# Output-gate columns turned a block later, one tile of queries instead of two, and other costs in the plan of a Fourier and neighbourhood-attention block

## The chip, the cores and the metric

One core of a Trainium2 chip runs the whole kernel in one launch. The metric is the device time in microseconds (us). The kernel before was timed three times; the profile and the trace come from one further, profiled execution.

## The reference

One layer of a diffusion backbone over 1024 positions of width 1024, with 256 context tokens; float32 throughout.

```python
xn = rms_norm(x, g) * (1 + sc_x) + sh_x          # shift, scale and gate from c through w_ada
cn = rms_norm(ctx, g) * (1 + sc_c) + sh_c
f_in, f_gate, q, k, v, na_gate = split(xn @ w_in)
q, k = rms_norm per head of q and k              # 8 heads of 64
f_out  = real(fft2(f_in, positions x channels)) @ w_four * silu(f_gate)
na_out = softmax([window scores + bias, scores on 256 context keys]) @ [v, vc] * silu(na_gate)
out = x + g_x * (concat(f_out, na_out) @ w_out)
```

The scores are taken as q times k in a higher precision than one pass of the matrix engine gives: a value is split into a high part and a low part that both fit the engine's fast 32-bit format, and the products high by high, low by high and high by low are added.

## The kernel before

TensorE (PE) does nearly all products in that split form, so that most of them come as three matmuls. The work runs in these stages:

- **Front** (L235 to L450): x is normalised, turned and modulated; the Fourier gate's products (`pg`, L365) fill PE.
- **Fold stage** (L597 to L632): the Fourier transform over positions is folded. For each of eight blocks `i` of 128 channels, `fold_products(i)` issues the products of that block (L572 to L585), `next(mid)` issues the sums of a block that is `AHEAD` = 2 blocks later on DVE (VectorE) and ACT (ScalarE), and then `gains(n)` is called for the `n` that `GAINS[i]` lists. `gains` sums the output gate c by w_ada: its matmuls (`pgs`, L284) leave the sums of half the columns in four rows of a PSUM bank. At the last step of each half (n = 3 and n = 7) it also copies the bank to SBUF on ACT (`part`, L491), turns it into columns with four matmuls (`pgc`, L494, recorded as eight) and adds the bias on DVE (`gcol`, L496). `gsum`, `pgc` and the next half's `gsum` use the same single bank, so that `gains(4)` comes behind `gcol`. The columns are needed only much later, in `gate_rows` (L1372).
- **Turn to columns** (`turn_columns`, L653): the folded sums are split by ACT and DVE (`ah`, `al`, L109 and L110; `a`, L663) and multiplied by tables (`pp`, L680 to L684). This begins right behind the fold stage.
- **Attention stage** (L1535 to L1590): this is laid out by a planner that runs while the program is built. It keeps a clock `now` and a list of when each engine is free, gives every operation a cost (for example `a_t(n)` for ACT and `d_t(n)` for DVE), and issues instructions in the order in which its own clock lets them start. That order is then fixed for each engine. Sequences for the Fourier rows, the context, the scores (`seq_rows`), the probabilities (`seq_scores`), their products with the values, and the queries and keys (`seq_build`) come first; wherever none of them can go on, one matmul of a long list (`feed`) is issued on PE: for each pair p of heads the projection `project(p)` (`pqkv`, L827), then the gate's `gate_proj(p)` (`png`, L849), and at the end the Fourier half of the output projection (`po`, L1447).
- **End** (L1592 on): the attention half of the output projection (`of`, L1623) and the sums with x (L1627).

What the change touches in the attention stage: `project` copies each projected tile out of PSUM and normalises q and k by head: squares on ACT, sums on DVE, a power on POOL (GpSimd; `n3`, L733), a product on DVE (`n4`, `raw`, L734). When the planner holds four tiles for done, `queries` and `keys` issue transposes on PE (`ptq` L903, `ptk` L917). `queries` then makes, for each head h, `qs1`: the high part in the head's own 64 partitions (ACT, L906) and the low part in the other 64 (DVE, L907); and `qs2`: a copy of the high part (DVE, L203), with zeros in the other 64 partitions. `ks1` holds the keys' high part in all 128 partitions; `ks2` the low part with zeros in the other 64. A tile of scores is `qs1` by `ks1` (L1171) plus `qs2` by `ks2` (L1173). `open_attention` allocates all this once the context is done, and sets the zeros: on POOL L977 and L978, L997, L1001, on DVE L980 to L994. `OP` and `OD` are what the planner holds POOL and DVE for meanwhile. `PRB` is the number of buffers for a tile of scores turned probabilities (`pr`); `EHB` that of the transposed and split probabilities (`eh`, `el`), and how many of their steps may wait for their products.

Of the kernel before, what the change touches and what calls it, by code (L numbers as in the profile page):

```python
# [11 lines left out]
F32 = mybir.dt.float32  # L12
R = mybir.dt.float32r
# [6 lines left out]
P = 128  # L20
# [3 lines left out]
TW, RT0, RT1, RT2, RH = 4, 0, 4, 4, 1  # L24
XS = (4, 8)
LAG, EB, TL = 1, 2, 0
AHEAD, GAINS = 2, ((0,), (1, 2), (3, 4), (5, 6), (7,), (), (), ())
S = dict(sem=0.13, rw=4, wo=2.6, rt=0, ri=12, rf=0, ro=1, ns=3, rr=2, rv=2)
WHO = dict(ml=(1, 0), ol=(0, 1), w=None, cw=(0, 1), ga=None, ce=(1, 0), el=(0,), vl=(0, 1), q2=(0,), kb=(0, 2), fm=None, wc=(2,), ec=(2,), oc=(0, 2), mc=(2, 0), cc=(2, 0), vc=(2,), fe=(0,), gc=(2,))
OP, OD, OC = 4.5, 2.0, 8.0  # L30
SEQ = 1024
CTX = 256
NB = 8
# [9 lines left out]
def tile_hybrid_block(  # L43
# [24 lines left out]
    act, dve, pool, pe = nc.scalar, nc.vector, nc.gpsimd, nc.tensor  # L68
    mm = pe.matmul

    def tap(name, t):
        if name in taps:
            nc.sync.dma_start(out=taps[name], in_=t)

    def f(t):
        return t.bitcast(F32)
# [107 lines left out]
    def a_t(n):  # L184
        return 0.09 + n * 0.00083

    def d_t(n):
        return 0.07 + n * 0.00104
# [11 lines left out]
    def copy_by(n, who, out, in_):  # L200

        both = ((DVE_, dve.tensor_copy, lambda n: 0.07 + n * 0.00052), (POOL_, pool.tensor_copy, p_t), (ACT_, act.copy, a_t))
        return [(e, time(n), lambda cp=cp: cp(out, in_)) for e, cp, time in (both[k] for k in who)]  # L203
# [265 lines left out]
                mm(o, g3[w][:, i], x[i][:, 512:1024], start=(i == 0 and n == 0), stop=(i == KT - 1 and n == 2))  # L469
        act.activation(gate_f[3][:, 512:1024], o, AF.Silu)  # L470

    gws, gsum = [], []

    def load_gains():

# [5 lines left out]
    def gains(n):  # L481
        hf, m = divmod(n, 4)
        if m == 0:
            gsum.append(bank("pgs", 2))
        o = gsum[hf]
        for k in range(2):
            condition(o, 2 * m + k, gws[n][:, k])
        if m < 3:
            return
        part = eop.tile([P, 512], F32, tag="s2", bufs=3, name="part")  # L490
        act.copy(part, o)  # L491
        gc = bank("pgc", 2)
        for j in range(4):
            mm(gc[:, j:j + 1], part[:, j * P:(j + 1) * P], pick[:, 0:1], start=True, stop=True)  # L494
        ks = slice(4 * hf, 4 * hf + 4)
        dve.tensor_tensor(out=gcol[:, ks], in0=gc[:, 0:4], in1=vec[:, V_BG + 4 * hf:V_BG + 4 * hf + 4], op=ALU.add)  # L496
# [92 lines left out]
    def load_table(n):  # L589
        kt, l = divmod(n, 2)  # L590
        t = pwp.tile([P, DM + 2], R, tag="wd", bufs=4, name="tab")
        pool.dma_start(out=t, in_=(tab_h, tab_l)[l][kt * P:(kt + 1) * P, :])
        (tbh, tbl)[l].append(t)
# [3 lines left out]
    with tc.manual_schedule(engines=MANUAL):  # L597
        fold_zero()
        for i in range(EB):
            fold_ends(i)  # L600
        mid = fold_middle()
        for _ in range(6 * AHEAD):
            next(mid)
        for j in range(4):
            fourier_gate(j)
        for n in range(8):
            fold_weights(n // 4, n % 4)
            if n > 3:
                load_gains()
            if n % 4 == 3:  # L610
                fold_nyquist(n // 4)
        last_gate()
        pe_0 = bank("p0", 0)
        pe_e = [bank(f"pe{m}", 1 - m % 2) for m in range(4)]
        pe_o = [bank(f"po{m}", 1 - m) for m in range(2)]
        for i in range(KT):
            fold_products(i)
            for _ in range(6):
                next(mid, 0)
            if i == 1:  # L620
                load_four()
            if i == 5:
                dve.tensor_tensor(out=wfr[0], in0=wfr[0], in1=wfr[1], op=ALU.add)
                dve.tensor_tensor(out=wfr[2], in0=wfr[2], in1=wfr[1], op=ALU.subtract)
            for n in GAINS[i]:
                gains(n)
                if n < 4:
                    load_gains()
                else:
                    load_table(n - 4)  # L630
    tap("gate_f", gate_f[1])
    st4.close()  # L632
    st1.close()
# [176 lines left out]
    def project(p):  # L810
        raws[p] = []
        for t in range(NB):
            while now[0] < banks[0]:
                yield None
            if t % 4 == 0:
                while p and not has(("v", p - 1, 0, t // 4), ("v", p - 1, 1, t // 4)):
                    yield None
                raw = rawp.tile([P, 4, 384], F32, tag="raw", name="raw")
                raws[p].append(raw)
            o = pj("pqkv")[:, 0:384]  # L820
            ts_ = slice(t * P, (t + 1) * P)
            for k in range(KT):
                while ("w", p, k) not in done:
                    yield None
                wh, wl = weights[p][k]
                for n, (x, w) in enumerate(((xnh, wh), (xnh, wl), (xnl, wh))):
                    mm(o, x[k][:, ts_], w, start=(k == 0 and n == 0), stop=(k == KT - 1 and n == 2))  # L827
                    yield 0.16
                if t == NB - 1 and p < 3:
                    prep(p + 1, k)  # L830
            rt = raw[:, t % 4]
            sqt = rawp.tile([P, 256], F32, tag="sqt", name="sqt")
            while t > 1 and ("raw", p, t - 2) not in done:
                yield None
            banks.append(1e9)
            banks.pop(0)
            n1, n2, n3, n4 = head_norm(rt[:, 0:256], sqt, 4)
            chain((ACT_, a_t(384), lambda rt=rt, o=o: act.copy(rt, o), 0),  # L838
                  lambda: banks.__setitem__(0 if banks[0] == 1e9 else 1, clock()),
                  (ACT_, a_t(256), n1), (DVE_, 0.42, n2), (POOL_, 0.96, n3), (DVE_, d_t(256), n4),  # L840
                  lambda t=t: done.__setitem__(("raw", p, t), 1), rank=S["rr"])

    def gate_proj(p):
# [54 lines left out]
    def queries(p, q):  # L898
        cs = slice(512 * q, 512 * q + 512)
        tbs[0] -= 1  # L900
        pq = tb("ptq")
        for j in range(4):
            pe.transpose(pq[:, j * P:(j + 1) * P], raws[p][q][:, j, 0:P], ident)  # L903
        for h in range(2):
            a, b = HALF[h], HALF[1 - h]
            chain((ACT_, a_t(512), lambda h=h, a=a: act.copy(qs1[h][a, cs], pq[a])),  # L906
                  (DVE_, d_t(512), lambda h=h, a=a, b=b: dve.tensor_tensor(out=qs1[h][b, cs], in0=pq[a], in1=f(qs1[h][a, cs]), op=ALU.subtract)),  # L907
                  lambda h=h: give() if h else None,
                  copy_by(512, WHO["q2"], qs2[h][a, cs], f(qs1[h][a, cs])),
                  lambda h=h: done.__setitem__(("q", p, h, q), 1), rank=h)  # L910

    def keys(p, c, cs, srcs):
# [44 lines left out]


    gts, att = ExitStack(), ExitStack()
    gtp = ap1 = ap2 = qs1 = qs2 = ks1 = ks2 = eye = rrow = sel = biases = trs = sms = None  # L960
    PRB, VSB = 5, 1

    def open_attention():
        nonlocal gtp, ap1, ap2, qs1, qs2, ks1, ks2, eye, rrow, sel, biases, trs, sms
        gfs.close()
        pqs.close()
        gst.close()
# [1 line left out]
        ap1 = att.enter_context(tc.tile_pool(name="ap1", bufs=1, **LT))  # L969
        ap2 = att.enter_context(tc.tile_pool(name="ap2", bufs=2, **LT))  # L970
        qs1 = [ap1.tile([P, SEQ], R, name=f"qs1{h}") for h in range(2)]
        qs2 = [ap1.tile([P, SEQ], R, name=f"qs2{h}") for h in range(2)]
        ks1 = [ap1.tile([P, SEQ + CTX], R, name=f"ks1{h}") for h in range(2)]
        ks2 = [ap1.tile([P, SEQ + CTX], R, name=f"ks2{h}") for h in range(2)]
        for h in range(2):
            b = HALF[1 - h]
            pool.memset(f(qs2[h])[b], 0.0)  # L977
            pool.memset(f(ks2[h])[b], 0.0)  # L978
        eye = ap1.tile([104, 8], F32, name="eye")
        dve.tensor_copy(eye, ident[0:104, 0:8])  # L980
# [177 lines left out]
    def row_max(p, h, t):  # L1158
# [8 lines left out]
        for z in range(2):  # L1167
            for o, kk in ((sl, lk), (sc, slice(SEQ, SEQ + CTX))):
                st, sp = (z == 0 and not (edge and o is sc)), (z == 1 and not (edge and o is sl))
                if z == 0:  # L1170
                    mm(o, qs1[h][:, ts_], ks1[h][:, kk], start=st, stop=sp)  # L1171
                else:
                    mm(o, qs2[h][:, ts_], ks2[h][:, kk], start=st, stop=sp)  # L1173
        now[0] += 2 * (nl + CTX) / 2400
        done["s", p, h, t] = 1
        pr = prs[p, h, t] = ap1.tile([P, 640], F32, tag="pr", bufs=PRB, name="pr")[:, 0:nl + CTX]
# [41 lines left out]


    STEPS = (10, 11, 0, 1, 2, 3, 12, 4, 13, 5, 6, 7)  # L1220
    EHB = 3
    pvs = {}

    def turned(p, h, t, kt):
# [324 lines left out]
    def feed():  # L1549
        for k in range(KT):  # L1550
            prep(0, k)
        prep_gate(0)
        for p in range(4):
            yield from project(p)
            if p == 3:
                wst.close()
                yield from gate_rows()
                side.append(out_loads())
            while "open" not in done:
                yield None  # L1560
            yield from gate_proj(p)
            if p < 3:
                prep_gate(p + 1)
        yield from out_fourier()
# [191 lines left out]
```

## Time and profile before

| what | value |
|---|---|
| median of 3 runs | 576.97 us |
| lowest and highest of them | 574.51 and 578.93 us |
| the profiled execution | 575.37 us |
| its span, first to last instruction | 573.6 us |
| matrix engine busy in the span | 546.6 us |
| VectorE, ScalarE, GpSimd busy | 388.5, 312.6, 139.9 us |

An engine's busy time is the union of its instructions. The records of consecutive matmuls overlap, because each is shown until its last result is out; the distance from start to start is what one costs. "Idle before, releaser" of an instruction is the time in which its engine had nothing running, and what it waited for.

### The profile page before, as it was taken

The numbers are of one execution on the slowest core, as the hardware profiler recorded it, in microseconds if no ns is written. First come the engines' busy times: TensorE is split into PE (matmuls) and PEld (weight loads), VectorE is DVE, ScalarE is ACT, GpSimd is POOL, SyncE is SP. The second block draws the span as 40 slices with busy tenths as digits, with TensorE's granted clock in tenths as the row PEclk, the third lists the DMA queues.
The fourth block names the chain that finished last, engine by engine and source line by source line (L and its number), as shares of the span: only waits on it lengthen the run. The fifth ranks groups of instructions, "written<-read, shape, count | busy, mean of one in ns | idle before, by whom it ended". The sixth has DMA issues, their size and how long they took to land.

```text
span 573.6 us, 9000 instructions
## 1 busy us (share of the span) xinstructions
PE 546.6 (95%) x3299; PEld 483.5 (84%) x3299; DVE 388.5 (68%) x801; ACT 312.6 (55%) x662; POOL 139.9 (24%) x144
## 2 busy tenths in 40 slices
PE   4899999999999899999999999999999898989997
PEld 3677896799878889999989999899998687868886
DVE  5774756686754868866678667777765978783142
ACT  6865462355665368764688646767456855520000
POOL 2200000115702533112431032411224513540000
PEclk9999999999999899999999999999999999999999
DMA  8991046426551521110221111220113556120052
GB/s 339 412 408 58 1 148 215 152 89 198 193 147 38 179 65 42 42 43 37 81 66 45 30 49 51 70 70 1 42 46 112 184 191 203 73 92 0 1 201 93
DMA packets 41459, 64.64 MB, mean 113 GB/s; under 512 B 3268, under 2 KB 25156, under 8 KB 40392
## 3 DMA queue, kind: packets, MB, share of 16 engines
q1 hardware_dynamic: 40408, 60.40, 31.1%
q0 software_dynamic: 1008, 3.67, 1.9%
q8 instruction: 26, 0.43, 0.3%
q14 instruction: 17, 0.14, 0.1%
HBM read 55.15 MB, written 8.91 MB: 112 GB/s over the span
## 4 chain that ended last, share of the span: by engine, by line
PE 75%; DVE 8%; ACT 6%; DMA 6%; issue 2%; POOL 2%; SPq 1%; POOLq 0%; DVEq 0%; ACTq 0%
PE pqkv L827 20%; PE of L1623 8%; PE pg L365 7%; PE po L1447 5%; PE st L1251 4%; PE png L849 4%; DMA wr<-in_w_in_dram 3%; PE s L1171 2%; PE s L1173 2%; PE pv L1285 2%; PE pv L1275 2%; DMA x<-in_xb_dram 2%; DMA owr<-in_w_out_dram 2%; PE pc L1133 1%; PE pw L502 1%
## 5 line engine op out<-in xcount | busy, mean ns | idle before, releaser
L827 PE MATMUL pqkv<-wl,xnh 128*128 128x384 f32 x256 | 88.3, 345 | 0.0
L827 PE MATMUL pqkv<-wh,xnl 128*128 128x384 f32 x256 | 88.0, 344 | 0.0
L827 PE MATMUL pqkv<-wh,xnh 128*128 128x384 f32 x256 | 87.8, 343 | 0.0
L733 POOL TENSOR_TENSOR hrs<-hss,mhalf 128x4 f32<-128x4 f32 (+1 forms) x34 | 36.7, 1082 | 149.2 <-DVE hss L730 145.8
L1262 DVE TENSOR_TENSOR el<-st,eh 128x512 fp32r<-128x512 f32 (+2 forms) x96 | 53.5, 572 | 17.0 <-ACT eh L1261 16.3
L1261 ACT CAST eh<-st 128x512 fp32r<-128x512 f32 (+2 forms) x96 | 47.0, 494 | 29.4 <-PE st L1251 25.9
L1183 ACT ACTIVATE pr<-pr,tr 128x640 f32<-128x640 f32 (+1 forms) x64 | 51.5, 805 | 15.4 <-DVE tr L1179 15.1
L1179 DVE CUSTOM_DVE_ANT_0 pr<-s,bias 128x640 f32<-128x640 f32 (+1 forms) x64 | 50.2, 784 | 10.6 <-PE s L1173 10.2
L827 PEld LDWEIGHTS pqkv<-wh,xnh 128*128 128x128 f32 x256 | 48.7, 190 | 0.6
L827 PEld LDWEIGHTS pqkv<-wl,xnh 128*128 128x128 f32 x256 | 48.6, 190 | 0.5
L827 PEld LDWEIGHTS pqkv<-wh,xnl 128*128 128x128 f32 x256 | 48.6, 190 | 0.4
L1251 PE MATMUL st<-ident,pr 128*128 128x128 f32 x304 | 47.3, 272 | 0.1
L1251 PEld LDWEIGHTS st<-ident,pr 128*128 128x128 f32 x304 | 37.0, 140 | 2.8 <-DVE el L1262 0.5
L1447 PE MATMUL po<-oh,mh 128*128 128x512 f32 x88 | 31.0, 396 | 3.0 <-DVE y L1453 1.5
L1627 DVE TENSOR_TENSOR y<-y,of 128x512 f32<-128x512 f32 (+1 forms) x17 | 11.1, 656 | 32.3 <-PE of L1623 32.3
L1171 PE MATMUL s<-ks,qs 128*128 128x256 f32 (+1 forms) x128 | 29.9, 313 | 0.7 <-DVE tr L1179 0.7
L203 ACT CAST wh<-wr 128x384 fp32r<-128x384 f32 (+1 forms) x44 | 22.6, 539 | 12.7 <-DMA wr<-in_w_in_dram 10.6
L1173 PE MATMUL s<-ks,qs 128*128 128x256 f32 (+1 forms) x128 | 28.3, 302 | 0.0
L198 DVE TENSOR_TENSOR wl<-wr,wh 128x384 fp32r<-128x384 f32 (+1 forms) x29 | 21.5, 754 | 9.6 <-ACT wh L203 7.7
L198 POOL TENSOR_TENSOR wl<-wr,wh 128x384 fp32r<-128x384 f32 (+1 forms) x19 | 20.9, 1104 | 28.9 <-ACT wh L203 15.2
L365 PE MATMUL pg<-xnh,w 128*128 128x512 f32 x96 | 27.3, 406 | 0.0
L838 ACT COPY raw<-pqkv 128x384 f32<-128x384 f32 x32 | 15.3, 478 | 21.4 <-PE pqkv L827 21.1
(295 smaller groups left out, 1442.9 us busy)
## 6 DMA issues: line engine op xcount, KB each, us to landing
wd<-in_w_ada_b_dram SPq DMA_DIRECT2D x8, 1024.0 KB, 11.6
wr<-in_w_in_dram SPq DMA_DIRECT2D x40, 192.0 KB, 2.8
wr<-in_w_in_dram SPq DMA_DIRECT2D x24, 256.0 KB, 3.1
x<-in_xb_dram SPq DMA_DIRECT2D x8, 512.0 KB, 7.3
wdg<-in_w_ada_g_dram SPq DMA_DIRECT2D x8, 512.0 KB, 4.7
owr<-in_w_out_dram SPq DMA_DIRECT2D x16, 256.0 KB, 3.4
y<-in_xb_dram SPq DMA_DIRECT2D x8, 512.0 KB, 5.4
out_dram<-y SPq DMA_DIRECT2D x15, 256.0 KB, 2.1
```

Of the source, the lines that this page charges most:

```text
L198: return [(e, time(n), lambda eng=eng: eng.tensor_tensor(out=out, in0=in0, in1=in1, op=op)) for e, eng, time in (both[k] for k in who)]
L365: mm(pg[j][hf], wj, x[i][:, hs], start=(i == 0 and g == 0), stop=(i == KT - 1 and g == 2))
L827: mm(o, x[k][:, ts_], w, start=(k == 0 and n == 0), stop=(k == KT - 1 and n == 2))
L1171: mm(o, qs1[h][:, ts_], ks1[h][:, kk], start=st, stop=sp)
L1173: mm(o, qs2[h][:, ts_], ks2[h][:, kk], start=st, stop=sp)
L1179: dve.tensor_tensor_reduce(out=pr, in0=sv, in1=bt, scale=-1.0, scalar=3.0e38, op0=ALU.add, op1=ALU.min, accum_out=tr[:, t:t + 1])
L1183: (ACT_, a_t(nl + CTX) + 0.15, lambda: act.activation(pr, pr, AF.Exp, bias=tr[:, t:t + 1], scale=-1.0, accum_out=sm[:, t:t + 1]), 1),
L1251: pe.transpose(s[:, j * P:(j + 1) * P], turned(p, h, t, kt), ident)
L1261: chain((ACT_, a_t(m), lambda: act.copy(eh[:, w], s3)), (DVE_, d_t(m), lambda: dve.tensor_tensor(out=el[:, w], in0=s3, in1=f(eh)[:, w], op ...
L1262: (DVE_, d_t(m), lambda: dve.tensor_tensor(out=el[:, w], in0=s3, in1=f(eh)[:, w], op=ALU.subtract)), give,
L1447: mm(o, mf[k][m][:, ts_], wf[hf][k][w_], start=(k == 0 and n == 0), stop=(k == 3 and n == 2))
L1623: mm(o[:, cs], ma[k][m][:, ts_], w[:, cs], start=(k == 0 and n == 0), stop=(k == 3 and n == 2))
```

## The change

The two halves of `gains` are separated: the copy to SBUF stays behind the last sums of a half, and a new `gain_columns(hf)` does the turning and the bias. It is called for the first half at the end of block 3, ahead of `gains(4)`, and for the second half behind block 7. `GAINS` moves n = 4 from block 2 to block 3 and n = 6 from block 3 to block 4. `qs2` is gone, with its copies, its zeros and its memory, and the second product of the scores takes `qs1`. `PRB` goes from 5 to 6 and `EHB` from 3 to 4. The planner's costs: `OP` 4.5 to 3.5, `n3` 0.96 to 1.1, `n4` `d_t(256)` (that is 0.34) to 0.9. In `feed`, the wait of `gate_proj` for `open_attention` is gone.

```diff
-AHEAD, GAINS = 2, ((0,), (1, 2), (3, 4), (5, 6), (7,), (), (), ())
+AHEAD, GAINS = 2, ((0,), (1, 2), (3,), (4, 5), (6, 7), (), (), ())
-OP, OD, OC = 4.5, 2.0, 8.0
+OP, OD, OC = 3.5, 2.0, 8.0
...
             condition(o, 2 * m + k, gws[n][:, k])
-        if m < 3:
-            return
-        part = eop.tile([P, 512], F32, tag="s2", bufs=3, name="part")
-        act.copy(part, o)
+        if m == 3:
+            gpart.append(eop.tile([P, 512], F32, tag="s2", bufs=3, name="part"))
+            act.copy(gpart[hf], o)
+
+    def gain_columns(hf):
+
+        part = gpart[hf]
         gc = bank("pgc", 2)
         for j in range(4):
             mm(gc[:, j:j + 1], part[:, j * P:(j + 1) * P], pick[:, 0:1], start=True, stop=True)
...
             for n in GAINS[i]:
+                if n == 4:
+                    gain_columns(0)
                 gains(n)
...
+        gain_columns(1)
...
-                  (ACT_, a_t(256), n1), (DVE_, 0.42, n2), (POOL_, 0.96, n3), (DVE_, d_t(256), n4),
+                  (ACT_, a_t(256), n1), (DVE_, 0.42, n2), (POOL_, 1.1, n3), (DVE_, 0.9, n4),
...
-                  copy_by(512, WHO["q2"], qs2[h][a, cs], f(qs1[h][a, cs])),
...
-    PRB, VSB = 5, 1
+    PRB, VSB = 6, 1
...
-        qs2 = [ap1.tile([P, SEQ], R, name=f"qs2{h}") for h in range(2)]
...
-            pool.memset(f(qs2[h])[b], 0.0)
...
-                if z == 0:
-                    mm(o, qs1[h][:, ts_], ks1[h][:, kk], start=st, stop=sp)
-                else:
-                    mm(o, qs2[h][:, ts_], ks2[h][:, kk], start=st, stop=sp)
+                mm(o, qs1[h][:, ts_], (ks1, ks2)[z][h][:, kk], start=st, stop=sp)
...
-    EHB = 3
+    EHB = 4
...
-            while "open" not in done:
-                yield None
             yield from gate_proj(p)
```

## Rows read from the trace of the kernel before

**Rows 1.** The page: engines over the span (busy us, share, instructions).

```profile
PE 546.6 (95%) x3299; PEld 483.5 (84%) x3299; DVE 388.5 (68%) x801; ACT 312.6 (55%) x662; POOL 139.9 (24%) x144
```

**Rows 2.** The chain that ended last, its end (start us, us, what).

```profile
506.93 19.36 PE po L1447 x84
526.29 43.71 PE of L1623 x204
```

**Rows 3.** Waits of PE over the span (us in total, times, longest us).

```profile
PE pt L328 <- ACT x L341: 9.3, 2, 7.6
PE ptq L903 <- DVE raw L734: 3.8, 2, 2.4
PE pv L1275 <- DVE el L1262: 2.9, 4, 1.2
...
PE pgc L494 <- ACT part L491: 1.5, 2, 0.7
PE po L1447 <- DVE gate L855: 1.5, 1, 1.5
```

**Rows 4.** Timeline of PE, the second half's columns (start us, us, engine, line, op, [idle before]).

```profile
109.38 1.05 PE L494 MATMUL pgc<-pick,part 128*128 128x1 f32 x8 [0.74 <-ACT part L491]
110.30 0.28 PE L572 MATMUL p<-wab_h,x0h 128*2 128x260 f32 x1
```

**Rows 5.** Timeline of DVE, from the second half's columns to the first splits.

```profile
110.47 0.16 DVE L496 TENSOR_TENSOR gcol<-pgc,vec 128x4 f32<-128x4 f32 x1 [2.01 <-PE pgc L494]
110.55 0.75 DVE L553 TENSOR_TENSOR s<-ef 128x256 f32<-128x256 f32 x2
...
117.71 1.51 DVE L110 TENSOR_TENSOR al<-pe,ah 128x260 fp32r<-128x260 f32 x4 [0.50 <-ACT ah L109]
119.56 0.42 DVE L663 TENSOR_TENSOR a<-a0f,a 2x260 fp32r<-2x260 f32 x1 [0.33 <-ACT a L662]
```

**Rows 6.** Timeline of PE, first products behind the fold stage.

```profile
119.63 0.28 PE L680 MATMUL pp<-tab,ah 128*4 128x258 f32 x1
...
120.42 0.28 PE L684 MATMUL pp<-onesr,a 34*4 34x258 f32 x1
```

**Rows 7.** Timeline of PE: first pair's queries, last projections, the gate's first product.

```profile
191.19 0.49 PE L903 MATMUL ptq<-ident,raw 128*128 128x128 f32 x3
194.05 0.33 PE L903 MATMUL ptq<-ident,raw 128*128 128x128 f32 x1 [2.37 <-DVE raw L734]
...
205.70 0.33 PE L827 MATMUL pqkv<-wh,xnl 128*128 128x384 f32 x1
...
206.40 0.40 PE L849 MATMUL png<-xnh,gh 128*128 128x512 f32 x1
```

**Rows 8.** Windows: stretch; us; PE, PEld, DVE, ACT, POOL busy; granted clock; DMA share; GB/s.

```profile
195.00:198.00 3.00, 3.00 (x12) 3.00 (x12) 2.69 (x5) 1.27 (x2) 0.62 (x1) 0.55 0.41 118
...
430.00:460.00 30.00, 25.55 (x148) 21.66 (x147) 23.98 (x42) 21.93 (x44) 15.04 (x11) 1.00 0.42 141
```

**Rows 9.** Timeline of DVE in `open_attention`.

```profile
188.02 3.27 DVE L982 COPY eye<-ident 8x8 f32<-8x8 f32 x3
...
193.57 0.42 DVE L734 TENSOR_TENSOR raw<-raw,hrs 128x256 f32<-128x256 f32 x1
```

**Rows 10.** Timeline of POOL in `open_attention`.

```profile
188.21 0.95 POOL L977 MEMSET qs<- 64x1024 f32 x1
189.10 1.17 POOL L978 MEMSET ks<- 64x1280 f32 x1
...
192.95 0.19 POOL L1001 MEMSET tr<- 128x40 f32 x2
```

**Rows 11.** Timeline of PE, the last pair's second queries.

```profile
437.63 0.33 PE L903 MATMUL ptq<-ident,raw 128*128 128x128 f32 x1 [1.42 <-DVE raw L734]
```

**Rows 12.** Group by line on DVE (busy us, mean ns, idle before).

```profile
L203 DVE CAST qs<-qs 64x512 fp32r<-64x512 f32 x16 | 7.0, 441 | 0.1
```

**Rows 13.** Waits of PE from 430 to 510.

```profile
PE pv L1275 <- DVE el L1262: 2.3, 2, 1.2
```

More of the change, by code (lines that the diff above doesn't have):

```diff
@@ L470, in last_gate @@
         act.activation(gate_f[3][:, 512:1024], o, AF.Silu)
-    gws, gsum = [], []
+    gws, gsum, gpart = [], [], []
     def load_gains():
@@ L959, in tile_hybrid_block @@
     gts, att = ExitStack(), ExitStack()
-    gtp = ap1 = ap2 = qs1 = qs2 = ks1 = ks2 = eye = rrow = sel = biases = trs = sms = None
-    PRB, VSB = 5, 1
+    gtp = ap1 = ap2 = qs1 = ks1 = ks2 = eye = rrow = sel = biases = trs = sms = None
+    PRB, VSB = 6, 1
     def open_attention():
-        nonlocal gtp, ap1, ap2, qs1, qs2, ks1, ks2, eye, rrow, sel, biases, trs, sms
+        nonlocal gtp, ap1, ap2, qs1, ks1, ks2, eye, rrow, sel, biases, trs, sms
         gfs.close()
```

## The prediction

> **What bounds the kernel now.** I read the engine shares first: PE is busy for 546.6 of 573.6 us and no other engine for more than 388.5 [rows 1]. So PE's queue is the bound and the only question is what stops it. The end of the chain of waits says the same: from 506.93 to 570.00 it is nothing but PE products [rows 2]. Whatever stall goes ahead of that shortens the whole; a chain of the attention that ends earlier gains nothing by itself, because PE still has 19.36 us of `po` products to issue behind it. The change removes no matmul, so it can only gain from the 573.6 - 546.6 = 27.0 us in which PE stands. The list of PE's waits says where [rows 3]: 9.3 us are the wait for the first x, which the change does not touch. What it can touch is `ptq` behind `raw` (3.8), `pv` behind `el` (2.9), `pgc` behind `part` (1.5) and `po` behind the gate (1.5), together 9.7 us. One cost is not in that list: behind the longest `ptq` wait the granted clock was 0.55 over 3 us [rows 8].
>
> **The gate's columns.** In each half PE stands 0.74 us for ACT's copy (1.5 us in two waits) [rows 3, 4]. Behind the change the products of the next block cover that copy, so 0.74 us goes for the first half. The sums only change blocks, at no cost, the DMAs of the tables that `gains` issues on POOL's queue come up to one block later and are needed only behind block 7, and `gains(4)` still follows `gcol`. For the second half 0.74 goes as well, and the eight turning products, 110.30 - 109.38 = 0.92, move behind block 7. So the last fold product ends at 119.63 - 0.74 - 0.74 - 0.92 = 117.23, and the turning products run to 118.15. But the new order also puts `gcol` into DVE's queue, and there the splits `al` and then `a` are behind it. `gcol` started 1.09 us after the first turning product (109.38 to 110.47), and the next DVE instruction 0.08 later [rows 4, 5]: so `gcol` now starts at 118.32 and `al` at 118.40, where it was 117.71. With 1.51 for `al` and 0.42 for `a` [rows 5], `a` is ready at about 120.33, and the product that reads it, which started at 120.42 [rows 6], starts at about 120.35. Of 1.48 us of waits removed 0.1 is left. Ends: 1.5 gained, if DVE's order costs nothing, and 0.5 lost, if `a` comes 0.5 later than I reckon, as much as the idle time that DVE already has there before `al`. I take 0.1, since every link of the chain has a row.
>
> **One tile of queries.** The 16 copies go, 7.0 us of DVE at 441 ns [rows 12], and the two `qs2` zeros of 0.95 us on POOL [rows 10]. The matmuls that took `qs2` take `qs1` and keep their size, because `ks2` is zero where `qs1` has the low part. Where PE is supplied, which is all but the places of its waits [rows 3], the copies lie beside PE's own work and gain nothing. They count at two places.
>
> First, in `open_attention`. The tile that PE waits for from 191.19 on is multiplied by DVE only at 193.57, behind a block of small instructions that begins at 188.02 [rows 7, 9]. Three 8x8 copies in it took 3.27 us, to 191.29, beside the zeros on POOL; zeros of 0.95, 1.17 and 0.95 in a row from 188.21 end at the same time [rows 9, 10]. So the copies get through when the third zero is done. Without `qs2` the first three zeros are two of 1.17 and a `bias` one, for which 0.25 is left (192.95 less the four long ones is 0.5 for two), and end near 190.8: 0.5 sooner. The rest of the block took 193.57 - 191.29 = 2.28, part of it beside zeros too; I put 0.2 on that. So DVE's product comes 0.7 sooner. Ends: nothing, if the copies wait for all that POOL has, and 1.9, if DVE gains what POOL gains.
>
> The Trainium skill, page "SBUF — State Buffer", section "Who interferes with whom", says that a DVE copy in a 2-port mode and a GpSimd instruction lock each other out, whichever comes second for one whole instruction. By that the three copies would have ended at 190.3 (the first ahead of the zeros, the others behind one zero each), one zero earlier than the row has it [rows 9, 10], so the trace shows a longer lock. By the rule the copies would now end at 190.6 behind the second `ks2` zero, DVE would gain 0.9 instead of 0.7, and the sum would be 4.3.
>
> Second, in the last pair, where PE is idle for 30.00 - 25.55 = 4.45 us of 430 to 460 [rows 8]. Four copies are 1.76 us of DVE there. But ACT is as full as DVE (21.93 against 23.98 of 30 us), so DVE's saving mostly turns into waiting for ACT. Ends: 1.8 gained, all of it, and 1.0 lost, if the plan, which now holds the queries for done 0.47 earlier (0.34 for the copy and 0.13 for its semaphore), issues scores before their data. I take 0.5, and 0.3 more for the small `pv` waits of the pairs before, half of 2.9 less the 2.3 of the last pair [rows 3, 13].
>
> **The planner's costs.** `n4` was planned at 0.34 us and took 0.42 [rows 9]; planned at 0.9 it puts the transposes `ptq` 0.56 us later in the plan, behind 0.56/0.16 = 3.5 more projection matmuls. Four of them took 206.40 - 205.70 = 0.70 [rows 7], so 0.6 us of work stands where PE waited. `n3` adds 0.14 us where POOL is not held. In the first pair the wait of 2.37 [rows 7] falls by 0.6 + 0.7 = 1.3; I take 1.2. In the last pair the wait of 1.42 [rows 11] falls by 0.6. The clock: over 195 to 198 it was 0.55, which cost 3 x 0.45 = 1.4 us [rows 8]. The wait of 1.42 in the last pair left the clock at 1.00 over 430 to 460 [rows 11, 8], so a first-pair wait of 1.2 should do so too, and the 1.4 us comes back. Ends: 0, if the fall has another cause, and 1.6. I take 1.4.
>
> **What costs and gains nothing.** `OP` only says when the plan lets POOL go on; POOL's zeros took 192.95 + 0.19 - 188.21 = 4.9 us and will take 3.0, so 3.5 fits as 4.5 did. The wait removed from `feed` was never waited for: the queries, which need the opening, stand at 191.19 and the gate's first product at 206.40, right behind the last projection [rows 7]. That edit is worth 0 unless the opening moves by 15 us. The sixth `pr` and the fourth `eh`, `el` let the attention run further ahead, which only changes which PE work comes first; they take 2.5 + 4 KB of the 8 KB per partition that `qs2` leaves, so nothing is pushed out.
>
> **The sum.** 0.1 (columns) + 1.2 (first queries) + 1.4 (clock) + 0.6 (last queries) + 0.5 (last pair) + 0.3 (small waits) = 4.1 us. The profiled execution took 575.37 with a span of 573.6; it would be 571.3 with a span of 569.5. The median of the runs, 576.97, is 1.6 above it, within their spread (574.51 to 578.93), and I set the forecast against the median: 576.97 - 4.1 = 572.9. One per cent, about what a measurement of this kernel can tell from no change, is 5.8 us.
>
> **The rivals.**
> A: the first wait stays. If the new plan lets the power `hrs` of the fourth tile slip behind POOL's zeros, DVE's `raw` is no earlier than now, the clock falls again, and 1.2 + 1.4 are not gained. For it: the order on POOL is the planner's and its costs changed. Against: the power is done before the zeros now and its cost rises by only 0.14. Time: 576.97 - 1.5 = 575.5.
> B: slower, through the last pair. The plan holds queries for done earlier, and with six and four buffers it puts more reductions and splits ahead of one another; DVE (23.98 of 30 us) and ACT (21.93) are already full there [rows 8], and PE, which takes its instructions in order, stands behind `el` and the gate. For it: that is what the waits of 2.3 (`pv`) and 1.5 (`po`) are now [rows 3, 13]. Against: the copies leave DVE and `n4` is planned too long. If the idle time of 4.45 doubles and the 0.5 is not gained, the time is 576.97 - 3.6 + 4.45 = 577.8; it decides from 3.6 us of new waiting on.
> C: more than forecast. The splits are not held up by `gcol` (1.4 more) and the last pair's waits for `el` and the gate (2.3 + 1.5 = 3.8) go too, 3.3 more than the 0.5 taken: 572.9 - 4.7 = 568.2. For it: `n4` and the copies together give the plan 2 to 3 us per pair of room. Against: ACT in the last pair, and the queue of DVE in the fold stage.
> D: the change does not do what it says: the gate's products do not wait for the attention now. That is in the sum as 0.
>
> **How the numbers follow.** Forecast 0.50, A 0.20, B 0.12, C 0.18. The forecast's own range is 570.5 to 575 (clock or not, last pair between -1 and +1.8). The range of 8 in 10 runs from 567.5 (a little past C) to 578 (B). Faster by over 1% means under 571.2: most of C (0.16) and the lower part of the forecast (0.15), 0.31. Slower by over 1% means over 582.7: B with twice its price, 0.04. The rest, 0.65, is within 1%.
>
> **What would show it.** In the fold stage: no wait of `pgc` for `part`; `gcol` of the second half directly ahead of `al`, and `al` at about 1.2 us behind the end of the last fold product. In the first pair: the wait of `ptq` at 0.9 to 1.5 us and the granted clock at 1.00 behind it. In the last pair: `ptq` under 1 us, and the sum of its waits for `el` and the gate at about 3.3. Busy PE within 2 us of 546.6, DVE down by about 7 us. Wrong I would be if the clock falls again, if `al` does not wait for `gcol`, or if a wait of over 2 us stands at a place where there was none.

## The result, and the profile after

The changed kernel took 571.18 us (median of 4 runs, 567.38 to 572.41) beside 576.94 for the kernel before on the same chip: a ratio of 0.988, 95% interval 0.984 to 0.992, so 5.8 us faster (4.5 to 9.1). The forecast was 572.9. Timed again later, beside 576.11, it took 570.11: 0.989 (0.986 to 0.993).

The profiled execution took 572.41 us with a span of 570.6, only 3.0 us under the one of before. Its engine shares and granted clock, from the page:

```profile
PE 546.2 (96%) x3299; PEld 485.0 (85%) x3299; DVE 377.6 (66%) x788; ACT 311.2 (55%) x659; POOL 140.4 (25%) x142
...
PEclk9899999899999999999999999999999989999999
```

There are three falls of the clock in it: near 20 us, near 105 and near 457. A second profiled execution of the same kernel took 567.87 us, and its page has no fall:

```profile
PE 542.7 (96%) x3299; PEld 481.9 (85%) x3299; DVE 377.5 (67%) x788; ACT 311.5 (55%) x659; POOL 140.4 (25%) x142
...
PEclk9999999999999999999999999999999999999999
```

PE is 3.5 us less busy there with the same instructions. So stages are compared below only where the clock is known. The waits of PE in the first profiled execution, to be held against [rows 3]:

```profile
PE pt L328 <- ACT x L341: 10.4, 3, 7.6
PE pgs L284 <- issue: 1.6, 1, 1.6
...
PE s L1173 <- DVE tr L1179: 1.3, 2, 1.0
...
PE pv L1285 <- DVE el L1262: 1.1, 1, 1.1
PE ptq L909 <- DVE raw L740: 1.1, 2, 0.7
PE pv L1275 <- DVE el L1262: 1.0, 1, 1.0
PE pp L690 <- POOL p L664: 0.8, 1, 0.8
```

`pgc` behind `part` (1.5) and `po` behind the gate (1.5) are gone, `ptq` fell from 3.8 to 1.1. The two lines of `pv` behind `el` have 2.1 together, where before had 2.9; `s` behind `tr` (DVE's step that adds the bias to a tile of scores) rose from 0.7 to 1.3. Two waits are of a new kind, both in the fold stage: 1.6 ahead of `pgs` and 0.8 ahead of `pp`. PE's timeline at the places where the stages meet:

```profile
86.84 0.28 PE L575 MATMUL p<-wab_h,x0h 128*2 128x260 f32 x1
...
102.42 0.95 PE L497 MATMUL pgc<-pick,part 128*128 128x1 f32 x8
...
105.01 1.57 PE L284 MATMUL pgs<-wdg,ccol 128*32 128x512 f32 x8 [1.64 <-issue]
...
121.86 0.28 PE L686 MATMUL pp<-tab,ah 128*4 128x258 f32 x1
...
123.57 0.28 PE L690 MATMUL pp<-onesr,a 34*4 34x258 f32 x1 [0.84 <-POOL p L664]
...
195.13 0.49 PE L909 MATMUL ptq<-ident,raw 128*128 128x128 f32 x3
...
196.32 0.33 PE L909 MATMUL ptq<-ident,raw 128*128 128x128 f32 x1 [0.70 <-DVE raw L740]
...
206.54 0.40 PE L855 MATMUL png<-xnh,gh 128*128 128x512 f32 x1
...
415.42 0.60 PE L909 MATMUL ptq<-ident,raw 128*128 128x128 f32 x4
...
435.13 0.33 PE L909 MATMUL ptq<-ident,raw 128*128 128x128 f32 x1 [0.36 <-DVE raw L740]
...
523.40 0.39 PE L1621 MATMUL of<-oh,mh 128*128 128x512 f32 x1
```

From such starts the time splits as follows (us; (c) marks a stage in which the granted clock fell below 0.9 for some 3 us; the best version is an experiment further down):

| stage, from PE's start to start | before | after | after, second execution | best version |
|---|---|---|---|---|
| span's start to the first fold product `p` | 84.64 | 86.84 (c) | 85.40 | 85.38 |
| to the first `pp` by `onesr`: fold stage | 35.78 | 36.73 (c) | 35.19 | 33.02 |
| to the first `png`: context, first projection and queries | 85.98 (c) | 82.97 | 83.02 | 83.36 |
| to the last pair's first `ptq`: the pairs between | 210.54 | 208.88 | 208.87 | 209.64 |
| to the first `of`: the last pair | 109.19 | 107.98 (c) | 106.39 | 106.33 |
| `of` to PE's end | 43.86 | 43.86 | 43.86 | 43.86 |

The first line of the table is ahead of everything that the change touches and varies by itself. Without it the second execution is 8.0 us shorter than the one of before: 0.6 in the fold stage, 3.0 to the gate's products, 1.7 in the pairs, 2.8 in the last pair. Some of the 3.0 is the fall of the clock that only the profile of before has there.

### The profile page after: what moved, and what is told of

Same layout as the page of the kernel before. It is cut to its first block, busy times and chain, and to the rows that moved or that the text cites. A ratio compares the mean times of both kernels' runs of the same rounds, so it can differ in the third digit from the quotient of the medians.

```text
span 570.6 us, 8972 instructions
## 1 busy us (share of the span) xinstructions
PE 546.2 (96%) x3299; PEld 485.0 (85%) x3299; DVE 377.6 (66%) x788; ACT 311.2 (55%) x659; POOL 140.4 (25%) x142
## 4 chain that ended last, share of the span: by engine, by line
PE 81%; DVE 6%; DMA 4%; ACT 3%; issue 2%; POOL 2%; SPq 1%; POOLq 0%; ACTq 0%; DVEq 0%
PE pqkv L833 20%; PE of L1621 8%; PE pg L365 7%; PE s L1173 6%; PE png L855 6%; PE st L1251 6%; PE po L1447 5%; PE pv L1285 3%; PE pv L1275 2%; DMA wr<-in_w_in_dram 2%; DMA x<-in_xb_dram 2%; PE pc L1136 1%; PE pw L505 1%; PE ada L284 1%; PE pc L1135 1%
## 5 line engine op out<-in xcount | busy, mean ns | idle before, releaser
L833 PE MATMUL pqkv<-wh,xnl 128*128 128x384 f32 x256 | 86.8, 339 | 0.0
L1173 PE MATMUL s<-ks,qs 128*128 128x256 f32 (+1 forms) x256 | 48.0, 309 | 1.3 <-DVE tr L1179 1.3
L1173 PEld LDWEIGHTS s<-ks,qs 128*128 128x128 f32 x256 | 39.5, 188 | 4.0 <-DVE tr L1179 3.0
L198 POOL TENSOR_TENSOR wl<-wr,wh 128x384 fp32r<-128x384 f32 (+1 forms) x19 | 22.1, 1166 | 27.3 <-ACT wh L203 22.5
L1447 PE MATMUL po<-oh,ml 128*128 128x512 f32 x64 | 26.0, 406 | 0.0
```

Of the source, the lines that this page charges most:

```text
L1173: mm(o, qs1[h][:, ts_], (ks1, ks2)[z][h][:, kk], start=st, stop=sp)
L1447: mm(o, mf[k][m][:, ts_], wf[hf][k][w_], start=(k == 0 and n == 0), stop=(k == 3 and n == 2))
```

## Experiments

"Gains" below is the move of the gate's columns, "costs" are `OP`, `n3` and `n4`, "buffers" `PRB` and `EHB`.

### The gate's columns undone, and alone

From the changed kernel:

```diff
-AHEAD, GAINS = 2, ((0,), (1, 2), (3,), (4, 5), (6, 7), (), (), ())
+AHEAD, GAINS = 2, ((0,), (1, 2), (3, 4), (5, 6), (7,), (), (), ())
...
-        if m == 3:
-            gpart.append(eop.tile([P, 512], F32, tag="s2", bufs=3, name="part"))
-            act.copy(gpart[hf], o)
-    def gain_columns(hf):
-        part = gpart[hf]
+        if m < 3:
+            return
+        part = eop.tile([P, 512], F32, tag="s2", bufs=3, name="part")
+        act.copy(part, o)
...
-                if n == 4:
-                    gain_columns(0)
...
-        gain_columns(1)
```

> The changed kernel with the old gains and the old GAINS, all else as changed. Theory: the new order of the gate's columns costs more than it removes, by two waits that come from reused memory. From the first fold product to the first product that reads the zero row (L684 of before, L690 of the changed kernel) the profile of before has 35.79 us and that of the changed kernel 36.72. So here 35.8, and a time 0.9 us under the changed kernel's. Rival: the new order gains what it removes (1.5 us) and the loss in the one profile is chance; then 1.5 us above the changed kernel's.

The reverse of this diff, put into the kernel before:

> The kernel before with the new gains and GAINS alone. Theory (reused memory): the same stretch takes 36.7 instead of 35.8 us, PE stands about 1.6 us ahead of the sums of n = 4 and about 0.8 us ahead of the product that reads the zero row; the time is 0.9 us above that of before, everything behind as before. Rival (it gains 1.5): the stretch takes 34.3 and the time falls by 1.5 us.

Undone: 569.64 us, 0.989 (0.987 to 0.992). Alone: 576.26, 0.999 (0.997 to 1.002). So by time this part is worth nothing that can be measured. By the stage table it is worth 0.6 us: the fold stage has 35.78 before and 35.19 with the new order alone, no fall in either. Both expectations missed that: they took the 36.73 of the first profile for the cost of the order, and that stage has a fall of the clock in it. (With the order undone the stage took 37.34, also with a fall, so that profile can't be used here.) The two new waits were as expected. They are in the timeline after:

```profile
103.47 0.76 DVE L556 TENSOR_TENSOR s<-xrt 128x256 f32<-128x256 f32 x2 [1.64 <-PE pgc L497]
104.15 0.68 DVE L562 TENSOR_TENSOR l<-s,h 128x512 fp32r<-128x512 f32 x1
104.75 0.15 DVE L499 TENSOR_TENSOR gcol<-pgc,vec 128x4 f32<-128x4 f32 x1
...
119.14 1.50 DVE L110 TENSOR_TENSOR al<-pe,ah 128x260 fp32r<-128x260 f32 x4 [0.50 <-ACT ah L109]
...
122.04 0.16 DVE L499 TENSOR_TENSOR gcol<-pgc,vec 128x4 f32<-128x4 f32 x1 [1.39 <-PE pgc L497]
...
122.07 0.31 POOL L661 MEMSET a<- 64x260 f32 x1 [8.91 <-PE pgc L497]
122.10 0.38 ACT L667 ACTIVATE a0f<-p 2x260 f32<-2x260 f32 x1 [1.91 <-PE pgc L497]
...
123.00 0.42 DVE L669 TENSOR_TENSOR a<-a0f,a 2x260 fp32r<-2x260 f32 x1 [0.80 <-ACT a L668]
```

In the first half `part` is one of three buffers of the tag `s2`, and now holds it a block longer. The next fold sum `s` needs that buffer and waits for `pgc`; `gcol` is behind it and behind `l` on DVE; and the sums of `gains(4)` need the bank that `gcol` reads. So PE stands 1.64 us at 105.01, where it stood 0.25 before: 1.39 more, against the 0.74 saved. In the second half `gcol` is not ahead of `al`; it is behind, and `al` is not late. What is late is `a`: ACT's `a0f` and POOL's zeros have no data from `pgc`, yet both are released by it. Both write memory laid out anew where `part` lay. That was a theory so far, and the next kernel tests it.

Together the new waits are 2.2 us longer than the old ones of the same places, more than the 1.48 us that the order removes. The stage is shorter all the same, because the sums themselves take less. From the trace before, one step of the sums (n = 4) and two in one block (n = 5 and 6), each with the fold product behind it:

```profile
99.26 1.05 PE L284 MATMUL pgs<-wdg,ccol 128*32 128x512 f32 x4 [0.25 <-DVE gcol L496]
100.24 0.28 PE L572 MATMUL p<-wab_h,x0h 128*2 128x260 f32 x1
...
103.42 1.06 PE L284 MATMUL pgs<-wdg,ccol 128*32 128x512 f32 x8
104.41 0.28 PE L572 MATMUL p<-wab_h,x0h 128*2 128x260 f32 x1
```

One step takes 0.98 us from start to start, and two steps whose sums go to different rows of the bank take 0.99. Before, the eight steps came in six such groups, since `pgc` stood between n = 3 and n = 4; with the new `GAINS` they come in five, (4, 5) and (6, 7) together. From start to start, waits left out, PE spends 6.06 us on the sums before and 4.95 with the new order (4.95 also in the kernel of the next section). So the 0.6 us are 1.1 us of sums and a few tenths at `pgc`, less the 0.7 by which the waits grew.

### The copy put into memory that nobody waits for

The same computation; `part` goes into a half of x's tile that has been read by then:

```diff
-            gpart.append(eop.tile([P, 512], F32, tag="s2", bufs=3, name="part"))
+            gpart.append(xrt[1][:, 1 + 2 * hf, 512:1024])
```

> The changed kernel with the two copies of the gate's sums in the half of x that the fold has already read, instead of in a buffer of the fold's sums. Theory (reused memory): DVE no longer waits for the turning products before it can write the fold's sums, and ACT and POOL no longer wait for them before they write the zero row's tiles; both new waits go, the first falls to the 0.3 us that the columns' sum takes, and the stretch takes about 34.4 us: 2.3 us less than the changed kernel and 1.4 less than before. My forecast's reason (the sum of the columns stands ahead of the splits on DVE): the first wait goes all the same, but the second stays, and the stretch takes about 35.2.

It took 567.92 us, 0.985 (0.983 to 0.988). The changed kernel was not run on that chip; all runs of this one (566.76 to 568.23) lie under all those of the kernel with the gains undone (568.82 to 571.96) on the same chip. Its timeline:

```profile
102.73 1.06 PE L284 MATMUL pgs<-wdg,ccol 128*32 128x512 f32 x8 [0.25 <-DVE gcol L499]
...
116.26 0.37 ACT L667 ACTIVATE a0f<-p 2x260 f32<-2x260 f32 x1
...
118.04 0.28 PE L686 MATMUL pp<-tab,ah 128*4 128x258 f32 x1
...
118.22 0.16 DVE L499 TENSOR_TENSOR gcol<-pgc,vec 128x4 f32<-128x4 f32 x1 [1.39 <-PE pgc L497]
118.41 0.42 DVE L669 TENSOR_TENSOR a<-a0f,a 2x260 fp32r<-2x260 f32 x1
...
118.97 0.27 PE L690 MATMUL pp<-onesr,a 34*4 34x258 f32 x1
```

`pgs` waits 0.25 instead of 1.64, `a0f` starts at 116.26, before the eight turning products (117.23 here) and not behind them, and the first product by `onesr` follows the first `pp` after 0.93 instead of 1.71. The fold stage is 33.02 us, 2.2 shorter than with the change as it was made (2.3 was expected, though from 36.73 to 34.4) and 2.8 shorter than before. Only the place of `part` differs, so the reused memory was the cause of both waits. What is left is `a`, which stands right behind `gcol` on DVE: the mechanism of the forecast, one instruction later than it had it.

### One tile of queries alone, the costs alone

One tile alone takes `qs2`, its copies and its zeros out of the kernel before:

```diff
-                  copy_by(512, WHO["q2"], qs2[h][a, cs], f(qs1[h][a, cs])),
...
-            pool.memset(f(qs2[h])[b], 0.0)
...
-                if z == 0:
-                    mm(o, qs1[h][:, ts_], ks1[h][:, kk], start=st, stop=sp)
-                else:
-                    mm(o, qs2[h][:, ts_], ks2[h][:, kk], start=st, stop=sp)
+                mm(o, qs1[h][:, ts_], (ks1, ks2)[z][h][:, kk], start=st, stop=sp)
```

> The kernel before with one tile of queries alone: no copies, no zeros for them, the buffers and the planner's costs as before. The first queries stand behind the same 135 projection matmuls as before, so any gain there comes from DVE being through the opening sooner. Theory: that is 1.1 us (5.75 us from its first copy to the product in before, 4.61 in the changed kernel), the wait of PE for the first queries falls from 2.4 to 1.2 us, the clock does not fall behind it, and the stage gains about 2.8 us of the 3.3. Rival: it is the planner's cost that matters, and the wait stays over 1.8 us with the clock falling.

The costs alone, again from the kernel before:

```diff
-OP, OD, OC = 4.5, 2.0, 8.0
+OP, OD, OC = 3.5, 2.0, 8.0
...
-(POOL_, 0.96, n3), (DVE_, d_t(256), n4),
+(POOL_, 1.1, n3), (DVE_, 0.9, n4),
```

> The kernel before with the planner's costs alone (OP 3.5, n3 1.1, n4 0.9); copies, zeros, buffers and gains as before. The first queries stand 3 projection matmuls later (138 instead of 135). Theory: the wait of PE for them falls by 0.5 us, from 2.4 to about 1.9, the stage gains 0.5 us, and 1.4 more if the clock does not fall behind it; over the pairs from the gate's first product to the last pair's queries the longer n4 takes the small waits away (1.5 us). Rival: the costs do nothing for the pairs, and that part stays at 210.5 us.

One tile alone: 572.26 us, 0.993 (0.991 to 0.996). Costs alone: 574.4, 0.995 (0.994 to 0.997). Each is faster by itself, by 4.7 and 2.9 us of the medians. By the ratios it is 3.9 and 2.7, together 6.6, beside 6.8 and 6.2 for the whole change: the times alone don't show that the parts overlap. The traces show it at one place. The wait of the first queries was 2.37 before, 1.22 with one tile and 1.59 with the costs (1.9 was expected), and the granted clock behind it was 1.00 in both profiled executions. So where a fall is there to be lost, only one of the parts can be paid for it. From the first `ga` product (at 128.15 before) to the first `png` the stage has 78.25 us before, 75.31 with one tile, 76.05 with the costs, 75.25 with all. In the pairs the costs alone gain 0.4 us, not the expected 1.5. In their last pair PE stands 4.54 us in one wait of `s` for `tr`, where before has 0.39 at most. Where one tile of queries is in as well, with the buffers of before or the new ones, no wait for `tr` is over 1.0.

### The costs, the zeros and the buffers taken back

Each from the changed kernel. The costs `n3` and `n4` of before, the other parts new (`OP` stays at 3.5):

```diff
-(POOL_, 1.1, n3), (DVE_, 0.9, n4),
+(POOL_, 0.96, n3), (DVE_, d_t(256), n4),
```

> The changed kernel with n3 and n4 planned as before (0.96 and 0.34). The first queries stand behind 135 projection matmuls again. Theory: PE waits 1.2 instead of 0.7 us there and about 0.9 instead of 0.4 for the last pair's, and the pairs between lose 1.5 us: the time is 2 to 3 us above the changed kernel's. Rival: the costs are worth only those 1.0 us.

Two more zeros on POOL, in the place and nearly of the size of those of `qs2`; the rest as in the changed kernel:

```diff
+            pool.memset(f(ks2[h])[b][:, 0:1024], 0.0)
             pool.memset(f(ks2[h])[b], 0.0)
```

> The changed kernel with two more zeros on POOL in the opening, as long as those of the second tile of queries were (they zero a part of the keys' low half a first time); nothing else, and the order on PE, DVE and ACT is the same. Theory: DVE's small copies stand behind POOL's zeros again, the product that the first queries wait for comes 1.1 us later, and PE waits 1.8 instead of 0.7 us there; the clock falls behind it or not. Rival: the zeros do not matter, the wait stays at 0.7.

The buffers of before:

```diff
-    PRB, VSB = 6, 1
+    PRB, VSB = 5, 1
...
-    EHB = 4
+    EHB = 3
```

> The changed kernel with five pr and three eh and el as before. Theory: the deeper buffers only change which of PE's work comes first, the time is the changed kernel's within 1 us and the waits of the last pair stay at about 4 us. Rival: it is the buffers that shortened the pairs (1.7 us from the gate's first product to the last pair's queries), and this is 1.7 us slower.

The three took 570.69 (0.988, 0.986 to 0.991), 570.01 (0.987, 0.984 to 0.991) and 569.05 us (0.986, 0.983 to 0.989): by time none differs from the changed kernel (0.988 and 0.989). The traces tell more. PE's wait for the first queries, where the changed kernel has 0.70, is first with the costs back, then with the zeros back:

```profile
194.85 0.33 PE L909 MATMUL ptq<-ident,raw 128*128 128x128 f32 x1 [1.21 <-DVE raw L740]
```

```profile
194.48 0.33 PE L909 MATMUL ptq<-ident,raw 128*128 128x128 f32 x1 [1.75 <-DVE raw L740]
```

So the zeros are worth 1.05 us of this wait and the costs 0.51; 2.37 less both leaves 0.81, and 0.70 was measured. The clock behind it was 1.00 in both. With the costs back the last queries wait 1.41 as before (0.9 was expected), the pairs between take 209.47 and the last pair 107.44 (no fall): the costs gain 0.6 and 1.05 us there, and not the 2 to 3 us in all that were expected. With the buffers back the pairs take 0.8 us more, yet the last pair 106.43 even with a fall in it; the kernel is no slower for it. So no gain of the buffers can be seen.

### The best version, and a way that failed

The copy in x's memory and the buffers of before, both diffs as above:

> The changed kernel with the gate's sums in the read half of x (as e5) and with five pr and three eh and el (as e6). Theory: the two are independent, since one is over before the planner begins; the fold stretch takes 33.0 us as in e5, from the gate's first product to the end's first 316.1 as in e6, and the time is about 567 us, 1 us under e5 and 2 us under e6. Rival: what e6 gained over the changed kernel was chance, and this is e5's time.

The changed kernel again, on the same chip:

> The changed kernel itself once more, beside e9 on one chip. Theory: 1.2% under before as the first time; the fold stretch takes 35.2 us where the clock does not fall in it and 36.7 where it does, and the wait for the first queries is 0.7 us with no fall behind it. Rival: the fall behind the first queries comes back in this execution, and the stage's gain of 3.3 us was partly chance.

And the best version with the context's operations planned at more:

```diff
-(POOL_, 0.46, n2), (DVE_, 0.67, n3), mark("xc", t)
+(POOL_, 0.9, n2), (DVE_, 1.2, n3), mark("xc", t)
```

> As e9, and the planner's costs of the context's normalisation nearer to what they take (POOL 0.46 to 0.9, DVE 0.67 to 1.2). Theory: planning what an operation really takes moves its reader behind more work, as it did for the queries: PE's wait of 1.1 us for the normalised context goes to about 0.2, and the time falls by up to 1 us against e9. Rival: the whole plan behind it shifts, and what is gained there is lost in the pairs.

The best version took 566.66 us (566.35 to 567.04): 0.983 (0.980 to 0.986) of the kernel before, and 3.5 us under the changed one (570.11, 567.87 to 571.04), with no run in common. The two profiled executions, in which the clock did not fall, have spans of 564.9 and 566.1: 1.2 of the 3.5 us, the 2.2 of the fold stage less what the stages behind it give back. Most of the other 2.3 goes with the clock: none of the six runs of the best version has a mean clock under 0.997, five of the six of the changed kernel have 0.990 to 0.997. Why it falls less often there is not shown; with the copy in x's memory alone the six runs had 0.994 to 0.997. With the context planned at more, the time went back to 570.57 (0.990): the wait for the normalised context went from 1.2 to 0.3, as expected, but the plan then has the first queries' product `raw` late, and PE stands 2.98 us for it.

## Why the prediction was right, and where not

**The total.** Forecast 4.1 us, measured 5.8 and 6.0: right in sign, inside the range, on the edge between "within 1%" and "faster by over 1%". The terms were less good than their sum, and that the sum came near is in part luck: the term of 1.4 for the clock is not in the measured time, and the terms behind `png` together were three times too small. One premise was wrong too, that the change can only gain from the 27.0 us in which PE stands: 1.1 us came from sums that take PE less time, and 1.3 more from PE's busy time behind `png`.

**The gate's columns** (forecast 0.1, measured 0.6 in the trace and nothing in the time). The size was near, the step was wrong. It said that `gcol` stands ahead of `al` on DVE and delays it; `gcol` came behind `al`, and `al` was not delayed, which was one of the forecast's own signs of being wrong. The 1.48 us were given back, with 0.7 more, by two other ways: in the first half by a buffer that is held longer, which the forecast did not price, and in the second by memory that is reused. The copy moved elsewhere showed both. And "the sums only change blocks, at no cost" put a gain at nothing: the steps now come in five groups and not six, 1.1 us. So the 0.6 is near 0.1 by two errors that nearly cancel.

**The first queries** (1.2 forecast; 2.37 - 0.70 = 1.67 measured). Right in mechanism. From the first opening copy to `raw` DVE took 193.57 - 187.82 = 5.75 us before; the first copy before, and the block after:

```profile
187.82 0.16 DVE L980 COPY eye<-ident 104x8 f32<-104x8 f32 x1
```

```profile
191.24 0.17 DVE L983 COPY eye<-ident 104x8 f32<-104x8 f32 x1
...
191.44 2.60 DVE L985 COPY eye<-ident 8x8 f32<-8x8 f32 x3
...
195.85 0.42 DVE L740 TENSOR_TENSOR raw<-raw,hrs 128x256 f32<-128x256 f32 x1
```

That is 4.61: 1.14 sooner, where 0.7 was said. 0.67 of it is in the three copies (3.27 to 2.60), where 0.5 was said, and 0.47 in what follows them, where 0.2 was said. Singly the copies took 0.16, 2.10 and 0.99 before, and 0.16, 1.20 and 1.21 after: before, the second stood beside two zeros (0.95 and 1.17) and the third beside one; after, each of them beside one zero of 1.17, and the third zero (`bias`) that the forecast added was not waited for. With two zeros put back the copies took only 2.39, and it was the `sel` copies behind them that took longer, 1.65 us for 0.39. By the rule of the Trainium skill, page "SBUF — State Buffer", section "Who interferes with whom", it was 0.9; nearer, but also short. The planner's move was forecast as 3.5 projection matmuls and is three: 138 instead of 135 stand ahead of the first `ptq`.

**The clock** (1.4). At this place as forecast: the windows right before and behind the wait, against 0.55 in [rows 8]:

```profile
193.00:196.00 3.00, 2.62 (x17) 2.35 (x15) 2.79 (x13) 0.14 (x1) 1.69 (x5) 1.00 0.91 250
196.00:199.00 3.00, 2.68 (x17) 2.68 (x18) 2.43 (x6) 1.95 (x4) 1.01 (x1) 1.00 0.97 299
```

Wait and clock together were forecast at 2.6 and are 3.0 in the stage. But the 1.4 us are not in the measured total: over all runs the changed kernel's clock is no higher than that of before. On the last chip the mean granted clock is 0.995 over 11 runs of before (0.988 to 1.000) and 0.995 over six of the changed kernel (0.990 to 1.000). The runs at 1.000 are 573.13, 574.20 and 574.79 us before and 567.87 after, 5.3 to 6.9 apart: the whole gain is there without any fall of the clock to undo. In the first profile after the clock stayed up here and fell at three other places. Of the timed kernels, one tile alone has a higher clock than before on its chip (0.997 to 1.000 in six runs, mean 0.9985 against 0.995), the costs alone do not (0.993 against 0.994).

**The last queries** (0.6). 1.42 to 0.36, so 1.06; with the costs of before 1.41. The costs do it, as said.

**The last pair and the small waits** (0.5 and 0.3). This is the term that was mis-sized. With the last queries, 1.4 us were forecast from `png` to `of`; 319.73 less 315.26 is 4.5. Before and in the second execution after, the windows of the four stages from `png` on (us; PE, PEld, DVE, ACT, POOL busy; clock; DMA):

```profile
206.40:267.69 61.29, 61.16 (x395) 57.80 (x395) 47.89 (x108) 43.80 (x100) 15.66 (x17) 1.00 0.16 45
267.69:341.62 73.93, 73.64 (x472) 70.52 (x471) 54.65 (x122) 49.63 (x112) 20.52 (x22) 1.00 0.18 53
341.62:416.94 75.32, 74.78 (x476) 71.03 (x475) 55.98 (x124) 49.24 (x111) 19.51 (x22) 1.00 0.17 52
416.94:526.13 109.19, 101.77 (x565) 87.94 (x564) 82.08 (x146) 57.45 (x115) 39.95 (x30) 1.00 0.34 118
```

```profile
203.61:264.70 61.09, 61.09 (x397) 57.97 (x396) 47.11 (x108) 43.32 (x99) 14.93 (x16) 1.00 0.18 54
264.70:338.61 73.91, 73.91 (x475) 71.23 (x474) 51.91 (x120) 49.02 (x112) 19.84 (x21) 1.00 0.16 47
338.61:412.48 73.87, 73.87 (x475) 71.27 (x474) 51.11 (x121) 49.60 (x112) 19.44 (x20) 1.00 0.18 53
412.48:518.87 106.39, 101.22 (x560) 87.02 (x559) 81.04 (x142) 56.62 (x113) 42.71 (x31) 1.00 0.35 120
```

PE stood 0.96 us in the pairs and 7.42 in the last; now nothing and 5.17: 3.2 us. The other 1.3 is busy time, which the list of PE's waits doesn't hold. I read the small waits from that list alone (2.9 for `el`); the same list for PE's weight loads, from 206 us on, had 4.2 for this line of `pv` alone:

```profile
PEld pv L1275 <- DVE el L1262: 4.2, 4, 1.5
```

In the second execution after, that is 1.3, and none of it lies in the pairs. The other line of `pv` (L1285) went from 0.8 to 1.5 there, `s` behind `tr` from 2.1 to 3.0. In the pairs alone the weight loads waited 2.7 us before and 0.4 after, where PE's own list has 0.6 and nothing: the weight loads' list was the nearer guide to the 1.7 us that the pairs gained. The last pair is separated by the runs (109.19 before, 107.61 with one tile alone, 107.44 without the costs, 106.39 with all); how the 1.7 of the pairs divides is not: of the three parts run alone none gives more than 0.4 (the buffers were not run alone). The bound of "all of it", 1.8 for the copies, was nearer than my 0.5: one tile alone gains 1.6 there, where the wait of `po` for the gate falls from 1.5 to 0.2. That ACT is as full as DVE did not hold it back.

**At nothing.** The wait in `feed` was not run by itself. In both kernels PE's order has the first queries, which need the opening, ahead of the gate's first product (191.19 and 206.40 before, 195.13 and 206.54 after), so the opening was always done when that wait was reached. The buffers were put at nothing, and no gain of theirs can be seen. DVE fell by 10.9 us, not 7: beside the copies' 7.0, the 29 low parts `wl` (L198) fell from 754 to 659 ns of mean, 2.6 us, which was not counted.

**The rivals.** A fell (`raw` is sooner, the clock is up). B fell: the waits for `el` and the gate are 2.1, not 3.8. C's time was nearest in the second execution but not by its mechanism: the gate's wait went, that for `el` shrank by 0.8 in PE's list, and the fold stage gave only half a microsecond. D was right.

## What to carry to other kernels

When a product is issued later, its operand is held longer: ask which ring of buffers it sits in, who is next in that ring, and what is laid into its memory when the pool closes; here that made PE stand longer than before the move, and a place that nobody waits for gained 2.2 us. When small matmuls move, ask which of them now stand side by side: two steps of the sums took the time of one. Read the waits of the weight loads beside those of the matmuls before a small wait is priced. Before a fall of the clock in one profile is priced, look at the mean clock of all the runs: here it was the same before and after.

## What was not expected of the hardware

Much of the spread of the runs goes with the clock. The six executions of the changed kernel on the last chip go in order of their mean granted clock: 567.87 us at 1.000, 568.77 at 0.997, 569.98 and 570.23 at 0.994, 570.40 at 0.993 and 571.04 at 0.990, about 1 us for each 0.003. Other kernels are less strict: with the copy in x's memory a run at 0.996 took 566.76 us and one at 0.997 took 568.06. The falls are not tied to one wait. In the fold stage the clock was 0.74 and 0.69 over 104 to 110 us in the first profiled execution after and 1.00 at the same place in the second, with the same waits of 1.6 and 0.8 us. And it did not fall behind the wait of 2.98 us that the last experiment made, longer than the one of before; its windows:

```profile
191.00:194.00 3.00, 0.31 (x3) 0.31 (x4) 2.41 (x14) 0.00 (x0) 1.49 (x5) 1.00 0.87 254
194.00:197.00 3.00, 3.00 (x21) 3.00 (x19) 2.27 (x4) 2.87 (x6) 0.00 (x0) 1.00 0.79 231
```

PE was busy for 0.31 of 3 us and had the full clock behind it; before, 2.37 us of waiting were followed by 0.55 in the kernel before and again where the gains alone were new. What decides between them stays open: no run here tells it.
